# The opening of a decoder layer on one core: x's first row block in four transfers, weight casts on GpSimd, turning bank by bank, fewer products on ones, and one low weight computed earlier

## The chip, the core and the metric

The kernel runs on one core of one Trainium2 chip. Its engines work side by side and wait for each other by semaphores: TensorE (PE in the profile, with its weight loads as PEld), VectorE (DVE), ScalarE (ACT), GpSimd (POOL) and SyncE (SP), which issues most of the transfers; ScalarE and GpSimd issue some too. The metric is the device time of one execution in microseconds (us); the lower, the better.

## The reference: one hybrid decoder layer

One layer over 512 tokens of width 1024, all in float32. `u = rmsnorm(x)` is multiplied by a wide weight, and the product is split into the parts of three branches (dilated attention, causal pooling, a state-space scan) and their gates. The gated sum of the branches goes through `w_o` and onto x. A feed-forward part and a last norm end it:

```
u = rmsnorm(x, ln1_g)
proj = u @ w_in                                 # split into q, k, v, pool_in, z, xbc, dt_raw, gates
merged = gates[0] * y_a + gates[1] * y_b + gates[2] * y_c
x = x + merged @ w_o
h = causal_dwconv(rmsnorm(x, ln2_g) @ w_up)     # 2 x 2816 columns, 3 taps
x = x + (silu(a) * v) @ w_down                  # a and v are the two halves of h
return rmsnorm(x, final_g)
```

## The kernel before: split products, an opening by row blocks, orders written out by hand

**Products.** Every float32 factor is split into a high part (a rounded copy, tiles `wh`, `xh`, `uh`) and a low part (the rest, `wl`, `xl`, `ul`). A product is then three sums: high by high, low by high, high by low. `cast` makes the high part of a weight from the loaded tile `raw`, and `low` the low part: a subtraction on VectorE, line 217, 128x2048 numbers at a time.

**Order.** Each engine runs its instructions in the order in which the code writes them. `program` yields jobs, one for each piece of weights. While the body of a job runs, `prepare` makes the low part of the next job's weights, casts those of the one after and loads those after that. For a job marked `late`, `prepare` is not run ahead of the body but handed to it as a generator, `rest`: its first step is `low`, its second the cast and the load.

**The opening.** x is turned (its columns brought to the partitions) in four row blocks `tb` of 128 tokens. `load_x` loads a block in two halves `xin[tb, h]` of 512 columns. `turned` transposes the block's eight pieces of 128 columns with the unit matrix `eye`. Piece `k` goes to a PSUM tile: for blocks 0, 2 and 3 the pieces `k` and `k + 4` share one of four banks; block 1 has three tiles of its own (`uT1`, `first[2]`, `first[1]`). `split_x` reads each piece twice: ScalarE writes the high part `xh[k]` (line 1906) and VectorE the low part `xl[k]` (line 1907). The products with the first weight tile `raw0` start on blocks 0 and 1 together (256 tokens): `group(0, (HH,), 0, 256)` needs `xh` and the high part `h0`, the next group needs `xl`, and the groups with `LH` need `l0`, which GpSimd computes (`low0`). In profile rows these products have line 1918 and the names `pa<-xh,wh`, `pa<-xl,wh` and `pa<-xh,wl`. Ahead of the first transposition and behind those of block 1, `warm_up` puts products of a tile of ones with itself on TensorE, whose result nobody reads: `WARM` of them and `STILL` of them.

**The opening of the feed-forward part.** The first two jobs on `w_up` (`opening`, `half` 0 and 1) multiply the first 256 tokens while the norm of the last two row blocks is still under way. `late[0]` and `late[1]` are generators for row blocks 2 and 3: the rest of the norm (lines 475 to 483) and then `norm_turn` (transpositions, line 457; `uh` on ScalarE, line 460; `ul` on VectorE, line 461).

Of the kernel before, what the change touches and what calls it, by code (L numbers as in the profile page):

```python
# [16 lines left out]
P = 128  # L17
S = 512
D = 1024
KD = D // P  # L20
# [62 lines left out]
def trunk(ctx: ExitStack, tc, out, x, rel_bias, ln1_g, w_in, b_gate, w_a, pool_w, pool_scale, w_b,  # L83
# [3 lines left out]
    act, dve, pool, pe, sp = nc.scalar, nc.vector, nc.gpsimd, nc.tensor, nc.sync  # L87

    x, w_in, w_a, w_b, w_c, w_o = x[0], w_in[0], w_a[0], w_b[0], w_c[0], w_o[0]
# [16 lines left out]
    def T(name, dt=F32, shape=(P, S)):  # L106
        return big.tile(list(shape), dt, name=name, tag="t")

    def MM(name):
        return psum.tile([P, S], F32, name=name, tag="mm")  # L110

    def SM(name):
        return psum.tile([P, S], F32, name=name, tag="sm")

    def small(name, shape, dt=F32):
        return tiny.tile(list(shape), dt, name=name, tag="tiny")
# [38 lines left out]
    def step():  # L155
        flush()
        if waiting:
            running.append(iter(waiting.pop(0)))
        now = [(it, 0) for it in running]
        for phase in (0, ROWS, WHOLE, REST):  # L160
            now = [(it, advance(it, phase) if at == phase else at) for it, at in now]
# [65 lines left out]
    def wsrc(w, k0, k1, c0, c1):  # L227
        return w[k0 * P:k1 * P, c0:c1].rearrange("(k p) c -> p k c", p=P)
# [14 lines left out]
    def chunk_a(ps, ws, j, xh, xl, ks, lo=0, hi=S, k0=0):  # L243
        wh, wl = ws
        mm3(ps[:, lo:hi], lambda k: wh[:, k0 + k, j * P:(j + 1) * P],
            lambda k: wl[:, k0 + k, j * P:(j + 1) * P],
            lambda k: xh(k)[:, lo:hi], lambda k: xl(k)[:, lo:hi], ks)
# [1204 lines left out]
    def up_evac(m, ps):  # L1452
        t = HC[m] = T("hc")
        act.activation(t, ps, AF.Identity, bias=ff["c1"][:, ff["b"] + m:ff["b"] + m + 1], scale=fw(2, m))  # L1454
        for k in range(2):
            sh = 2 - k
            dve.scalar_tensor_tensor(t[:, sh:], ps[:, :S - sh], fw(k, m), t[:, sh:], OP.mult, OP.add)  # L1457
        if m < KF:
            act.activation(t, t, AF.Silu)  # L1459
            return  # L1460
        a = HC[m - KF]
        pool.tensor_tensor(a, a, t, OP.mult)  # L1462

        def later():
            yield
            k = m - KF
            if k % 2:
                h, l = T("fh", F32R), T("fl", F32R)
                act.copy(h, a)
                it = sums_of(HC[k - 1], a, T("sah", F32R), T("sal", F32R),  # L1470
                             lambda j, h, l: FS.__setitem__((j, k // 2), (h, l)), k >= KS)
                next(it)
                dve.tensor_sub(l, a, h.bitcast(F32))
                ACTS[k] = (h, l)
                yield
                for _ in it:
                    yield
                return
            t = T("f0", F32R)
            act.copy(t[:, :256], a[:, :256])  # L1480
            dve.tensor_sub(t[:, 256:], a[:, :256], t[:, :256].bitcast(F32))
            FS[0, k // 2] = (t[:, :256], t[:, 256:])

        running.append(later())
# [61 lines left out]
    def up_jobs():  # L1546
        held, rest = [], []

        def opening(job, half):
            def body(ws):  # L1550
                uh2, ul2 = nxt["uh"], nxt["ul"]
                if half == 0:
                    rest.append(job.prepare(later=True))
                    next(late[1])
                pss = [MM("pu") for _ in range(2)]

                def product(a, b, i):
                    for j in range(2):
                        for k in range(KD):
                            pe.matmul(pss[j][:, :256], a[:, k, j * P:(j + 1) * P], b[:, k, :256],  # L1560
                                      start=i + k == 0, stop=i == 2 and k == KD - 1)

                product(ws[0], uh2, 0)
                product(ws[0], ul2, 1)
                if half == 0:
                    product(ws[1], uh2, 2)
                next(late.pop(0), None)

                next(rest[0], None)
                if half:  # L1570
                    product(ws[1], uh2, 2)
                for j in range(2):
                    held.append((ws, j, pss[j], KF * half + j))
                if half == 0:
                    return
                for n, (ws_, j, ps, m) in enumerate(held):
                    chunk_a(ps, ws_, j, lambda k: uh2[:, k, :], lambda k: ul2[:, k, :], range(KD), 256, S)
                    if n == 1:
                        job.prepare()
                    up_evac(m, ps)  # L1580
                    step()
            return body

        for p in range(KF // 2):
            for half in range(2):
                def body(ws, p=p, half=half):
                    uh2, ul2 = nxt["uh"], nxt["ul"]
                    for j in range(2):
                        ps = MM("pu")
                        chunk_a(ps, ws, j, lambda k: uh2[:, k, :], lambda k: ul2[:, k, :], range(KD))  # L1590
                        up_evac(KF * half + 2 * p + j, ps)
                        step()
                c = half * DFF + p * 256
                job = Job([wsrc(w_up, 0, KD, c, c + 256)], KD, 256, body)
                if p == 0:
                    job.late = True
                    job.body = opening(job, half)
                yield job
# [233 lines left out]
    xin, warm = {}, small("warm", [P, 1])  # L1832

    def load_x(tb, engs=(sp, sp)):
        for h in range(2):
            t = xin[tb, h] = T("xin")
            engs[h].dma_start(t, x[tb * P:(tb + 1) * P, h * S:(h + 1) * S])
# [1 line left out]
    g8, g1 = T("g8"), cpool.tile([P, KD], F32, name="g1")  # L1839
    act.dma_start(g8[:KD, :P], ln1_g[0].rearrange("(k p) -> k p", p=P))  # L1840
    sp.dma_start(eye, c_eye)
    load_x(0, (act, sp))
    dve.memset(ones.bitcast(F32), 1.0)
    dve.memset(eps, EPS)
    dve.memset(both, 0.0)
# [11 lines left out]
    raw0 = w0.raw = wraw.tile([P, KD, 256], F32, name="raw", tag="raw")  # L1857
# [19 lines left out]
    h0 = w0.high = whp.tile([P, KD, 256], F32R, name="wh", tag="wh")  # L1877
# [3 lines left out]
    def part(j, k0, k1):  # L1881
        return slice(None), slice(k0, k1), slice(j * P, (j + 1) * P)

    def low0(j, k0, k1):
        o = part(j, k0, k1)
        pool.tensor_tensor(l0[o], raw0[o], h0[o].bitcast(F32), OP.subtract)
# [6 lines left out]
    def block(tb, k):  # L1893
        if tb == 1:
            return (uT1, first[2], first[1])[k % 3][:, (k // 3 + 1) * P:(k // 3 + 2) * P]
        return bank(k)[:, tb % 2 * P:tb % 2 * P + P]

    def turned(tb):
        if tb % 2 == 0:
            banks[:] = [SM("uT") for _ in range(4)]  # L1900
        for k in range(KD):
            pe.transpose(block(tb, k), xin[tb, k // 4][:, (k % 4) * P:(k % 4 + 1) * P], eye)

    def split_x(tb, k):
        c = slice(tb * P, (tb + 1) * P)
        act.mul(xh[k][:, c], block(tb, k), g1[:, k:k + 1])
        dve.scalar_tensor_tensor(xl[k][:, c], block(tb, k), g1[:, k:k + 1],
                                 xh[k][:, c].bitcast(F32), OP.mult, OP.subtract)
# [33 lines left out]
    warm_up(WARM)  # L1942
    pe.transpose(first[2][:, :KD], g8[:KD, :P], eye[:KD, :KD])
    turned(0)
    dve.tensor_copy(g1, first[2][:, :KD])
    for k in range(KD):
        split_x(0, k)
    turned(1)
    for k in range(KD):
        if k == 2:  # L1950
            for k0 in (0, 4):
                dve.tensor_copy(h0[part(0, k0, k0 + 4)], raw0[part(0, k0, k0 + 4)])
            low0(0, 0, KD)
        split_x(1, k)
    warm_up(STILL, 0)
    group(0, (HH,), 0, 256)
# [6 lines left out]
    half_squares(dve, 0, 1)  # L1963
    group(1, (HH,), 0, 256)
    turned(2)
    for k in range(KD):
        split_x(2, k)
# [79 lines left out]
AT = ((9, 10, 11, 12, 13, 14, 15), (17, 17, 18, 19, 20, 21, 22))  # L2047
MIX = "ZZ0zz1ggggwaa"
SSD_ORDER = ((0, 0, 1), (1, 0, 1), (0, 1, 1), (2, 0, 1), (1, 1, 1), (3, 0, 1), (2, 1, 1), (3, 1, 1))
WARM, STILL = 10, 7  # L2050

# [1 line left out]
_INS = ['x', 'rel_bias', 'ln1_g', 'w_in', 'b_gate', 'w_a', 'pool_w', 'pool_scale', 'w_b',  # L2053
# [26 lines left out]
```

## Time and profile before

| | |
|---|---|
| median of 3 runs | 1012.55 us (1012.4 to 1013.15) |
| the profiled execution | 1012.54 us, its span 1010.8 us |
| TensorE busy | 999.7 us, 99% of the span |
| VectorE, ScalarE, GpSimd busy | 753.7, 534.7 and 137.8 us |
| granted clock of TensorE over the span | 0.998 |

The profiled execution's own time is 1.7 us more than its span (what lies ahead of the first and behind the last instruction). It stands within 0.01 us of the median of the runs. A row of a timeline gives the start, the time from the first start to the last end of the merged instructions, the engine, the line, what is written from what, and, in brackets, the time for which the engine sat idle before it and who ended that.

### The profile page before, as it was taken

Reading aid. Unit: us, or ns where it says so; the run is one execution under the profiler, and the core shown is the slowest. Engines: PE = TensorE matmul, PEld = TensorE weight load, DVE = VectorE, ACT = ScalarE, POOL = GpSimd, SP = SyncE. Lnnn points to the kernel's source line nnn. Section 1 sums busy time; section 2 is a strip of 40 time slices with the busy share of each in tenths; the row PEclk is TensorE's granted clock in tenths of the full one; section 3 lists DMA queues with packets and bytes.
Section 4 is the critical chain, followed back from the end, with each engine's and each line's share of the span. In section 5 each row is a group of like instructions: output and inputs, shape, how many; then the busy total and the mean of one; then the engine's idle time right before and its main releaser. Section 6 shows DMA issues by size and latency. Waiting matters only on the chain.

```text
span 1010.8 us, 13607 instructions
## 1 busy us (share of the span) xinstructions
PE 999.7 (99%) x5307; PEld 850.0 (84%) x5307; DVE 753.7 (75%) x962; ACT 534.7 (53%) x929; POOL 137.8 (14%) x111
## 2 busy tenths in 40 slices
PE   9999999999999999999999999999999999999996
PEld 8898878999988888888888888898888888888885
DVE  6995668677767645776889888868778768685877
ACT  6343546554445566888566246554444434443456
POOL 4400010110000000000044501302111100121032
PEclk9999999999999999999999999999999999999999
DMA  7344360755343435552254754232352134542573
GB/s 221 102 126 131 106 187 4 193 150 147 102 155 94 108 100 132 146 137 62 77 152 125 211 188 90 80 126 84 99 193 84 50 117 149 175 115 73 146 184 109
DMA packets 117735, 127.03 MB, mean 126 GB/s; under 512 B 6791, under 2 KB 96462, under 8 KB 117671
## 3 DMA queue, kind: packets, MB, share of 16 engines
q1 hardware_dynamic: 112327, 116.98, 37.4%
q0 software_dynamic: 5040, 8.65, 5.4%
q8 instruction: 42, 0.69, 0.3%
q10 hardware_dynamic: 304, 0.53, 0.1%
q14 instruction: 22, 0.18, 0.1%
HBM read 121.56 MB, written 3.00 MB: 123 GB/s over the span
## 4 chain that ended last, share of the span: by engine, by line
PE 96%; DVE 2%; ACT 0%; DMA 0%; issue 0%; ACTq 0%
PE pa L239 37%; PE pu L239 23%; PE pb L239 10%; PE pd L239 8%; PE pqk L239 6%; PE pq L239 3%; PE ps L810 1%; PE pa L1918 1%; PE ppw L239 1%; PE po L858 1%; PE pt L844 1%; PE py L1140 1%; DVE wl L217 1%; PE pyo L1147 1%; PE pst L1128 0%; DMA xin<-in_x_dram 0%
## 5 line engine op out<-in xcount | busy, mean ns | idle before, releaser
L217 DVE TENSOR_TENSOR wl<-raw,wh 128x2048 fp32r<-128x2048 f32 (+3 forms) x86 | 205.9, 2396 | 32.9 <-ACT wh L195 24.2
L195 ACT CAST wh<-raw 128x1024 fp32r<-128x1024 f32 (+2 forms) x168 | 167.0, 1011 | 53.0 <-DVE raw L362 17.8
L1457 DVE SCALAR_TENSOR_TENSOR hc<-pu,fcol,hc 128x510 f32<-128x510 f32 x88 | 65.9, 748 | 53.7 <-ACT hc L1454 52.0
L239 PE MATMUL pu<-uh,wh 128*128 128x512 f32 (+1 forms) x352 | 83.6, 379 | 0.0
L239 PE MATMUL pu<-uh,wl 128*128 128x512 f32 (+1 forms) x352 | 83.5, 379 | 0.0
L239 PE MATMUL pu<-ul,wh 128*128 128x512 f32 (+1 forms) x352 | 83.5, 379 | 0.0
L239 PE MATMUL pa<-uh,wh 128*128 128x512 f32 (+1 forms) x336 | 80.9, 380 | 0.0
L239 PE MATMUL pa<-ul,wh 128*128 128x512 f32 (+1 forms) x336 | 78.9, 374 | 0.0
L239 PE MATMUL pa<-uh,wl 128*128 128x512 f32 (+1 forms) x336 | 78.8, 374 | 0.0
L239 PEld LDWEIGHTS pu<-ul,wh 128*128 128x128 f32 x352 | 64.2, 188 | 12.5
L239 PEld LDWEIGHTS pu<-uh,wl 128*128 128x128 f32 x352 | 64.2, 188 | 12.4
L239 PEld LDWEIGHTS pu<-uh,wh 128*128 128x128 f32 x352 | 64.1, 188 | 12.4
L1454 ACT ACTIVATE hc<-pu,fcol,fcol 128x512 f32<-128x512 f32 x40 | 31.2, 779 | 75.7 <-PE pu L239 75.7
L239 PEld LDWEIGHTS pa<-ul,wh 128*128 128x128 f32 x336 | 60.7, 188 | 11.4
L239 PEld LDWEIGHTS pa<-uh,wl 128*128 128x128 f32 x336 | 60.7, 188 | 11.2
L239 PEld LDWEIGHTS pa<-uh,wh 128*128 128x128 f32 x336 | 59.4, 189 | 10.6
L1462 POOL TENSOR_TENSOR hc<-hc 128x512 f32<-128x512 f32 x22 | 29.9, 1360 | 279.0 <-DVE hc L1457 243.3
L217 DVE TENSOR_TENSOR wl<-w,wh 128x2048 fp32r<-128x2048 f32 (+1 forms) x26 | 54.3, 2088 | 9.8 <-issue 4.5
L195 ACT CAST wh<-w 128x1024 fp32r<-128x1024 f32 (+1 forms) x52 | 47.2, 950 | 8.6 <-DMA w<-in_ffn_w_down_dram 3.8
L832 ACT ACTIVATE sb<-sb,nmls 128x128 f32<-128x128 f32 (+1 forms) x72 | 30.0, 418 | 32.5 <-DVE nmls L829 21.9
L1459 ACT ACTIVATE hc<-hc 128x512 f32<-128x512 f32 x22 | 13.9, 633 | 40.3 <-DVE hc L1457 40.3
L1123 POOL TENSOR_TENSOR st<-st,dts 128x512 f32<-128x512 f32 x4 | 4.2, 1051 | 225.4 <-ACT st L1131 164.9
(461 smaller groups left out, 2012.8 us busy)
## 6 DMA issues: line engine op xcount, KB each, us to landing
raw<-in_w_in_dram SPq DMA_DIRECT2D x24, 1024.0 KB, 5.5
raw<-in_ffn_w_up_dram SPq DMA_DIRECT2D x22, 1024.0 KB, 5.1
raw<-in_w_in_dram SPq DMA_DIRECT2D x14, 512.0 KB, 4.0
raw<-in_w_in_dram SPq DMA_DIRECT2D x8, 768.0 KB
raw<-in_ffn_w_down_dram SPq DMA_DIRECT2D x6, 1024.0 KB, 4.9
raw<-in_w_b_dram SPq DMA_DIRECT2D x4, 1024.0 KB
al<-ad SPq DMA_DIRECT2D x16, 256.0 KB, 7.9
raw<-in_w_c_dram SPq DMA_DIRECT2D x4, 1024.0 KB, 5.3
```

Of the source, the lines that this page charges most:

```text
L195: (other.tensor_copy if other and i else act.copy)(job.high[:, :, o], job.raw[:, :, o])
L217: (eng or dve).tensor_tensor(l[:, :, o], job.raw[:, :, o], h[:, :, o].bitcast(F32), OP.subtract)
L239: pe.matmul(ps, l, r, start=first and n == 0, stop=last and n == total - 1, skip_group_check=onto)
L810: pe.matmul(pss[i][:, o:o + w * P], q[r, n * P:(n + 1) * P], k[r, kb * P:(kb + w) * P], start=True, stop=True)
L832: act.activation(sb[:, off:off + w * P], sb[:, off:off + w * P], AF.Exp, bias=nm[:, n, h:h + 1], accum_out=ls[:, n, h:h + 1])
L844: pe.transpose(pt[:, o:o + P], sb[:, o:o + P], eye)
L858: pe.matmul(po[DH * hh:DH * hh + DH, n * P:(n + 1) * P], V[g, kb + i][:, (2 * c + hh) * DH:(2 * c + hh + 1) * DH], probs[2 * c + hh, nb][: ...
L1140: pe.matmul(py[DH * i:DH * i + DH, j * P:(j + 1) * P], xc[:, o:o + DH], als[j // 2][:, lo:lo + P], start=True, stop=True)
L1454: act.activation(t, ps, AF.Identity, bias=ff["c1"][:, ff["b"] + m:ff["b"] + m + 1], scale=fw(2, m))
L1457: dve.scalar_tensor_tensor(t[:, sh:], ps[:, :S - sh], fw(k, m), t[:, sh:], OP.mult, OP.add)
L1459: act.activation(t, t, AF.Silu)
L1462: pool.tensor_tensor(a, a, t, OP.mult)
```

## The change

The edits of the opening: the two halves of x's row block 0 are each loaded in two transfers of 256 columns, first the first 256 columns of both halves, then the second, ScalarE issuing those of half 0 and SyncE those of half 1. `turned` goes through the pieces in the order 0, 4, 1, 5, 2, 6, 3, 7, so that the two pieces of a bank follow each other. The high part of the first half of `raw0` is made by GpSimd instead of VectorE, ahead of all of block 1's splitting. `WARM` goes from 10 to 7 and `STILL` from 7 to 4. In the feed-forward opening the first step of `rest` (the low part of the second job's weights) moves from behind the products of `half` 0 to ahead of them.

```
     if half == 0:
         rest.append(job.prepare(later=True))
+        next(rest[0])
         next(late[1])
...
     next(late.pop(0), None)
-    next(rest[0], None)
     if half:
+        next(rest[0], None)
         product(ws[1], uh2, 2)
...
-    load_x(0, (act, sp))
+    for c in (0, 256):
+        for h, eng in enumerate((act, sp)):
+            if c == 0:
+                xin[0, h] = T("xin")
+            eng.dma_start(xin[0, h][:, c:c + 256], x[:P, h * S + c:h * S + c + 256])
...
-        for k in range(KD):
+        for k in (0, 4, 1, 5, 2, 6, 3, 7):
             pe.transpose(block(tb, k), xin[tb, k // 4][:, (k % 4) * P:(k % 4 + 1) * P], eye)
...
     turned(1)
+    for k0 in (0, 4):
+        pool.tensor_copy(h0[part(0, k0, k0 + 4)], raw0[part(0, k0, k0 + 4)])
+    low0(0, 0, KD)
     for k in range(KD):
-        if k == 2:
-            for k0 in (0, 4):
-                dve.tensor_copy(h0[part(0, k0, k0 + 4)], raw0[part(0, k0, k0 + 4)])
-            low0(0, 0, KD)
         split_x(1, k)
...
-WARM, STILL = 10, 7
+WARM, STILL = 7, 4
```

TensorE at the start of the program, before (`uT` without a number and `pa` are PSUM tiles; `pa<-ones` are the products on ones; the last row is the first group of real products):

```order
L1854 MATMUL pa<-ones 128x128 x10
L1943 MATMUL pa<-eye,g_110 128x8
L1902 MATMUL uT<-eye,xin 128x128 x8
L1902 MATMUL uT_123<-eye,xin 128x128
L1902 MATMUL pa<-eye,xin 128x128 x2
L1902 MATMUL uT_123<-eye,xin 128x128
L1902 MATMUL pa<-eye,xin 128x128 x2
L1902 MATMUL uT_123<-eye,xin 128x128
L1902 MATMUL pa<-eye,xin 128x128
L1854 MATMUL pa<-ones 128x128 x7
L1918 MATMUL pa<-xh,wh 128x256 x8
```

and now (line numbers are 4 or 5 higher behind the new lines):

```order
L1859 MATMUL pa<-ones 128x128 x7
L1948 MATMUL pa<-eye,g_110 128x8
L1907 MATMUL uT<-eye,xin 128x128 x8
L1907 MATMUL uT_125<-eye,xin 128x128
L1907 MATMUL pa<-eye,xin 128x128 x4
L1907 MATMUL uT_125<-eye,xin 128x128 x2
L1907 MATMUL pa<-eye,xin 128x128
L1859 MATMUL pa<-ones 128x128 x4
L1923 MATMUL pa<-xh,wh 128x256 x8
```

Six products on ones are gone, and block 1's pieces come in the new order; nothing is moved past the first real products.

VectorE at the same place, before, from the splitting of block 0 (`uT`) to the first sum of squares (line 445):

```order
L1907 SCALAR_TENSOR_TENSOR xl<-uT,g_111,xh 128x128 x8
L1907 SCALAR_TENSOR_TENSOR xl<-uT_123,g_111,xh 128x128
L1907 SCALAR_TENSOR_TENSOR xl<-pa,g_111,xh 128x128
L1952 CAST wh<-raw 128x4x128 x2
L1907 SCALAR_TENSOR_TENSOR xl<-pa,g_111,xh 128x128
L1907 SCALAR_TENSOR_TENSOR xl<-uT_123,g_111,xh 128x128
L1907 SCALAR_TENSOR_TENSOR xl<-pa,g_111,xh 128x128 x2
```

and GpSimd now, from the barrier of the program's start on:

```order
L2080 UNCONDITIONAL_BRANCH
L1955 CAST wh<-raw 128x4x128 x2
L1891 ISA
L1891 TENSOR_TENSOR wl<-raw,wh 128x8x128 x2
L1977 TENSOR_TENSOR xf<-xh,xl 128x256 x8
```

The two casts left VectorE, where they stood between the second and the third piece of block 1, and are GpSimd's first work; GpSimd's subtractions (line 1886 before) stand behind them as they stood first before.

VectorE at the opening of the feed-forward part, before (`va`, `vo`, `v`, `r`, `rt` and `u` are row block 3's norm; the first `ul` row is row block 2's, the second row block 3's; line 217 is the low part of the second job's weights):

```order
L1330 TENSOR_SCALAR va_106<-so_105 128x1
L1331 TENSOR_SCALAR vo_107<-va_106 128x1
L475 SCALAR_TENSOR_TENSOR v<-ss,vo_107 128x1
L476 RECIPROCAL r<-sq 128x1
L477 SCALAR_TENSOR_TENSOR rt<-r,v 128x1
L478 SCALAR_TENSOR_TENSOR rt<-rt,r 128x1
L482 SCALAR_TENSOR_TENSOR u_5961<-x_5515,rt,grow 128x512
L461 TENSOR_TENSOR ul_5789<-uT,uh_5788 128x4x128 x2
L217 TENSOR_TENSOR wl<-raw,wh 128x2048
L461 TENSOR_TENSOR ul_5789<-uT,uh_5788 128x4x128 x2
```

and now:

```order
L1330 TENSOR_SCALAR va_106<-so_105 128x1
L1331 TENSOR_SCALAR vo_107<-va_106 128x1
L217 TENSOR_TENSOR wl<-raw,wh 128x2048
L475 SCALAR_TENSOR_TENSOR v<-ss,vo_107 128x1
L476 RECIPROCAL r<-sq 128x1
L477 SCALAR_TENSOR_TENSOR rt<-r,v 128x1
L478 SCALAR_TENSOR_TENSOR rt<-rt,r 128x1
L482 SCALAR_TENSOR_TENSOR u_5957<-x_5511,rt,grow 128x512
L461 TENSOR_TENSOR ul_5785<-uT,uh_5784 128x4x128 x4
```

The subtraction moved up past the rest of row block 3's norm and past row block 2's `ul`; TensorE's order there is unchanged.

## The prediction

> **What bounds the kernel now.** I read the page first (its busy times and the chain that ended last), then TensorE's waits, then the chain and the timeline of the opening.
>
> ```profile
> span 1010.8 us, 13607 instructions
> PE 999.7 (99%) x5307; PEld 850.0 (84%) x5307; DVE 753.7 (75%) x962; ACT 534.7 (53%) x929; POOL 137.8 (14%) x111
> PE 96%; DVE 2%; ACT 0%; DMA 0%; issue 0%; ACTq 0%
> ```
>
> TensorE is the bound from end to end: 96% of the chain, 11.1 us of the span not busy. TensorE's waits say where an edit can act at all (us in total, times, longest):
>
> ```profile
> PE pa L1854 <- DVE ones L1843: 1.1, 1, 1.1
> PE pa L1918 <- ACT xh L1906: 0.8, 1, 0.8
> PE pu L1560 <- DVE wl L217: 0.6, 1, 0.6
> PE uT L1902 <- DMA xin<-in_x_dram: 0.5, 1, 0.5
> ```
>
> There are four, and the change aims at the last three: two in the first 11 us, one in the feed-forward opening at 666 us. Between and behind them TensorE has work, so what is saved there should stay saved to the end. The chain through the opening (start, length):
>
> ```profile
> 1.36 4.20 DMA xin<-in_x_dram
> ...
> 5.61 0.78 PE uT L1902 x5
> ...
> 6.41 0.38 ACT xh L1906
> ...
> 6.81 2.68 DVE xl L1907 x10
> 9.49 0.67 DVE wh L1952 x2
> 10.16 0.27 DVE xl L1907
> ...
> 10.46 0.38 ACT xh L1906
> ...
> 10.88 2.80 PE pa L1918 x19
> ```
>
> x lands, five transpositions pass before the first split (bank 0 is full only with piece 4), and VectorE's two casts of the weights hold up the splits behind them: ScalarE's next piece waits for VectorE. The timeline of the same stretch shows where TensorE comes to run without a pause:
>
> ```profile
> 9.41 0.76 DVE L1952 CAST wh<-raw 128x512 fp32r<-128x512 f32 x2
> ...
> 9.97 1.81 PE L1918 MATMUL pa<-xh,wh 128*128 128x256 f32 x8 [0.83 <-ACT xh L1906]
> 10.24 5.20 POOL L1886 TENSOR_TENSOR wl<-raw,wh 128x1024 fp32r<-128x1024 f32 x2 [9.80 <-DVE wh L1952]
> ...
> 10.46 0.37 ACT L1906 ACTIVATE xh<-pa,g 128x128 fp32r<-128x128 f32 x1 [0.56 <-DVE xl L1907]
> ...
> 11.50 1.01 PEld L1918 LDWEIGHTS pa<-xl,wh 128*128 128x128 f32 x8
> ```
>
> The eight products of the first group take 1.53 us from 9.97 to 11.50, though eight weight loads of the next group take 1.01 (0.12 each). From 11.50 on TensorE is full. So the first gain is how much earlier than 11.50 the second group starts.
>
> **Term 1, the opening: 0.93 us.** Three chains must meet there: the splits, the high part h0, and x's low parts.
>
> The splits start earlier. Pieces 0, 4, 1, 5 need half of the bytes that they needed, and the first split waits for two transpositions instead of five. I estimate the first split at 5.2 (6.41 before): half of the 4.20 us of the DMA row is latency that stays, the rest halves. From the first split to the second group it took 11.50 - 6.41 = 5.09 us, of which 0.56 was ScalarE's wait behind the casts, now gone; so the second group could start by 9.73. The fewer products on ones only keep TensorE free for x: fourteen passes instead of twenty end near 4.2 to 4.5 at the pace of the start (row under the clock's rival).
>
> h0 is later than that. It needs raw0's first half, whose landing the change doesn't hasten:
>
> ```profile
> 2.60 1.06 SPq L1860 DMA_DIRECT2D raw<-in_w_in_dram  x2
> raw<-in_w_in_dram SPq DMA_DIRECT2D x2, 512.0 KB, 6.0
> 4.00:6.00 2.00, 1.45 (x13) 1.24 (x13) 0.17 (x1) 0.00 (x0) 0.00 (x0) 1.00 1.01 372
> L1837 SPq DMA_DIRECT2D xin<-in_x_dram x7: 421/431/2937, 1.2 to 7.6; - x7
> ```
>
> Issued at 2.60, it lands 6.0 later, at 8.60. SyncE now issues one transfer more ahead of it (0.43), and so all behind it on that queue, x's blocks 1 to 3 among them. But from 4 us on the DMA engines are full (share 1.01, 372 GB/s) and the same bytes stand in front, so I take 8.7, from 8.5 to 8.9. GpSimd waits for it with nothing else queued, casts 2 times 128x512, and the fifth product needs the second cast. The trace has no cast on GpSimd. Bounds (busy us, mean ns; then VectorE's own casts of this shape, min/median/max ns):
>
> ```profile
> L1123 POOL TENSOR_TENSOR st<-st,dts 128x512 f32<-128x512 f32 x4 | 4.2, 1051 | 225.4 <-ACT st L1131 164.9 <-PE pst L1128 34.5 <-DVE xs L1153 26.1
> L1321 POOL TENSOR_TENSOR xg<-x,grow 128x512 f32<-128x512 f32 x4 | 9.2, 2299 | 16.7 <-DVE x L1376 16.7
> L1952 DVE CAST wh<-raw x2: 419/421/423, 9.4 to 9.7; 128x512 fp32r<-128x512 f32 x2
> ```
>
> So a cast costs c between 0.42 (VectorE's) and 2.30 (GpSimd's dearest group of this size, two inputs, beside a busy VectorE). I take 0.70: 1.05 of the cheapest group moves two streams in and one out, the cast one in and one out, two thirds. It is nearest to that row, since in this stretch VectorE reads PSUM for half of its input. The second group then starts at 8.7 + 2 x 0.70 + 4 x 0.12 = 10.57, and the gain is 11.50 - 10.57 = 0.93; in general 2.33 - 2c.
>
> What moves behind it is covered: GpSimd's two subtractions start at 10.1 and take 5.20, so l0's second half is there at 15.3, and TensorE wants it at 17.41 less the gains, about 16.2 (row below). ScalarE's casts of raw0's second half wait for its landing as before.
>
> **Term 2, turning by banks: 0.31 us.** Two row blocks of eight transpositions each, and the group behind:
>
> ```profile
> 13.52 1.04 PE L1902 MATMUL uT<-eye,xin 128*128 128x128 f32 x8
> 16.30 1.35 PE L1902 MATMUL uT<-eye,xin 128*128 128x128 f32 x8
> 17.41 1.20 PE L1918 MATMUL pa<-xh,wl 128*128 128x256 f32 x8
> ```
>
> Block 3 takes 1.35 against block 2's 1.04: it writes into the banks that block 2's splits are still reading, and the order 0, 1, 2, 3 wants the fourth bank after three transpositions. The new order wants it after six (0.33 later), and block 2's splits start three transpositions earlier. The 0.31 should go entirely; it is hidden in busy time and in no list of waits.
>
> **Term 3, the low weights: 0.64 us.** The feed-forward opening:
>
> ```profile
> 660.31 0.15 DVE L1331 TENSOR_SCALAR vo<-va 128x1 f32<-128x1 f32 x1
> 661.00 0.16 DVE L475 SCALAR_TENSOR_TENSOR v<-ss,vo 128x1 f32<-128x1 f32 x1 [0.54 <-ACT junk L443]
> 661.98 0.75 DVE L482 SCALAR_TENSOR_TENSOR u<-x,rt,grow 128x512 f32<-128x512 f32 x1
> 662.66 1.05 ACT L460 CAST uh<-uT 128x512 fp32r<-128x512 f32 x2
> 664.47 2.28 DVE L217 TENSOR_TENSOR wl<-raw,wh 128x2048 fp32r<-128x2048 f32 x1
> 665.13 1.04 PE L457 MATMUL uT<-eye,u 128*128 128x128 f32 x8
> 666.80 2.18 PE L1560 MATMUL pu<-uh,wl 128*128 128x256 f32 x16 [0.64 <-DVE wl L217]
> 668.82 1.12 PE L239 MATMUL pu<-uh,wh 128*128 128x256 f32 x8
> ```
>
> The subtraction now runs from 660.5 to 662.8. Queued behind it on VectorE is row block 3's norm (475 to 482): it starts 1.7 later and ends at 664.4 instead of 662.73. The transpositions that need it come at 665.13: 0.7 to spare, and without that cover each us there would be a us lost. ScalarE's uh for row block 2 stands behind row block 3's scaling and ends near 665.5 instead of 663.7; TensorE reads it from 668.2 on. The four ul rows end near 667.6, wanted at 669.1. So the wait goes, and nothing is late next. Bounds: 0 (if something else holds) to 0.64.
>
> **Sum.** 0.93 + 0.31 + 0.64 = 1.88 us. The profiled execution took 1012.54, the median is 1012.55: 1012.54 - 1.88 = 1010.66, so 1010.7.
>
> **The rivals.** *GpSimd casts as fast as VectorE.* With c = 0.42 term 1 is 1.49, the sum 2.44, the time 1010.1. For it: a cast has one input, and GpSimd's rows above all have two. Against: nothing of GpSimd's here runs at VectorE's pace. "GPSIMD Engine Reference" of the Trainium skill, section "Engine selection", says that work with two inputs is about twice as slow there as on VectorE and with one input runs roughly at line rate; no row here shows one input.
>
> *GpSimd becomes the bound and the kernel slower.* h0 is now GpSimd's alone. The sum is 3.28 - 2c; from c = 1.64 on it is a loss. At the 2.30 of line 1321 h0 is complete at 13.3, the second group starts at 13.8, term 1 loses 2.27, and the time is 1013.9. For it: the row of line 1321. Against: that has two inputs, and line 1886 with two inputs takes 2.6 us for twice the columns in this very stretch.
>
> *The clock falls.* TensorE's pace on the products on ones, at the start and from 3.96 on:
>
> ```profile
> 1.06 2.50 PE L1854 MATMUL pa<-ones 128*128 128x128 f32 x10 [1.06 <-DVE ones L1843]
> 3.96 0.94 PE L1854 MATMUL pa<-ones 128*128 128x128 f32 x7
> ```
>
> Ten passes in 2.50 at the start, seven in 0.94 later: twice the pace, reached after some 2.9 us of steady work. With seven products the steady stretch is 3.1 to 3.5 us, and from there to 10 us TensorE pauses for longer than before. If the pace falls there, some 2.9 us of the real products go at half pace: a loss of 1.4, time 1012.1. Against: the pauses before (0.55, 0.83) did nothing, and none now should pass 1.5 us. "TensorE: Matmul & The Clock Gate" of the Trainium skill, part 1, says that the clock halves after an idle window of about 3.4 us and that the windows run free of the kernel's start; by this the seven products are a near thing and the pauses are not. This trace's 2.9 us agree with a window that had begun before the kernel.
>
> *The opening's gain is given back* at a later wait that the shift uncovers, and terms 2 and 3 alone stay: 1011.6. Against: the list of TensorE's waits names none between 11 and 660 us.
>
> **How the numbers follow.** A change of 0.2% is 2.0 us, about what a measurement of this kernel can tell from no change; the forecast lies just inside. The sum passes 2.0 for c below 0.63. My case (all three terms, c from 0.55 to 0.9, landing 8.5 to 8.9) has 0.50: times from 1010.2 to 1011.3, of it 0.22 beyond the bound and 0.28 within. Casts at VectorE's pace: 0.23, faster. GpSimd as the bound: 0.12, of it 0.08 within and 0.04 slower. The clock: 0.10, of it 0.07 within and 0.03 slower (two such stretches, or one with dear casts). Given back: 0.05, within. Faster 0.45, within 0.48, slower 0.07. The range runs from 1009.9 (casts at 0.42, landing at 8.5) to 1012.6 (the clock's 1012.1 with casts 0.25 dearer): only most of the GpSimd rival and the tail of the clock's lie above.
>
> **What would show it.** In the changed profile: GpSimd's cast rows of some 0.7 us from 8.7 on, the second group's weight loads near 10.6 instead of 11.50, with TensorE's only wait there on GpSimd; block 3's transpositions in 1.04; no wait of TensorE on line 217. The prediction is wrong if the casts take less than 0.5 or more than 1.0, if raw0 lands elsewhere than 8.5 to 8.9, if products of the first groups stand 0.2 apart, or if a wait of TensorE appears that is in no list of before.

## The result: 1.75 us faster, and the profile after

The changed kernel took 1011.08 us (median of 21 runs, 1010.25 to 1013.26), the kernel before 1012.83 (21 runs beside it, 1011.96 to 1013.89). The ratio is 0.9985, 95% interval 0.9979 to 0.9991: faster by 1.75 us, 0.17%, where 1.88 were forecast. Medians here and below are over all runs; the ratio is not the quotient of the two medians, which would be 0.9983.

The profiled execution took 1011.78 us, 0.70 more than that median; that of before lay 0.29 under its own. So the two profiles differ by 0.76 only, and I read them place by place. The page and TensorE's waits:

```profile
span 1010.0 us, 13587 instructions
PE 1000.0 (99%) x5295; PEld 850.4 (84%) x5295; DVE 754.0 (75%) x960; ACT 535.2 (53%) x929; POOL 137.7 (14%) x113
PE pa L1859 <- DVE ones L1848: 1.1, 1, 1.1
PE pa L1907 <- DVE xl L1912: 0.9, 1, 0.9
```

The waits on line 217 at the feed-forward opening and on the first transpositions are gone, but TensorE is not less busy: something runs slower. The timeline of the opening (start, first start to last end, engine, line):

```profile
4.54 2.20 PE L1907 MATMUL uT<-eye,xin 128*128 128x128 f32 x9
5.27 2.70 ACT L1911 ACTIVATE xh<-uT,g 128x128 fp32r<-128x128 f32 x8 [1.54 <-PE uT L1907]
7.65 1.08 PE L1907 MATMUL pa<-eye,xin 128*128 128x128 f32 x4 [0.91 <-DVE xl L1912]
9.17 1.77 PE L1859 MATMUL pa<-ones 128*128 128x128 f32 x8
9.20 0.37 ACT L1911 ACTIVATE xh<-uT,g 128x128 fp32r<-128x128 f32 x1 [1.24 <-PE uT L1907]
9.34 1.17 POOL L1955 CAST wh<-raw 128x512 fp32r<-128x512 f32 x2 [8.89 <-DMA raw<-in_w_in_dram]
10.67 1.02 PEld L1923 LDWEIGHTS pa<-xh,wh 128*128 128x128 f32 x8
11.04 0.36 ACT L1911 ACTIVATE xh<-pa,g 128x128 fp32r<-128x128 f32 x1
11.61 1.03 PEld L1923 LDWEIGHTS pa<-xl,wh 128*128 128x128 f32 x8
```

The first split comes at 5.27, 1.14 earlier than before, as planned, and GpSimd's two casts take 1.17 together. But block 1 of x is turned late, raw0 is there only at 9.34, and the second group starts at 11.61, later than the 11.50 of before. Eight passes on ones take 1.77, 0.22 apart, where 0.11 is the full pace: TensorE ran at half pace until 10.65 us. The row at 7.65 names VectorE as releaser, but VectorE's splits were then still under way; in the run e8_ones_0_0 below the same row, at 7.75, ends "[0.98 <-DMA xin<-in_x_dram]": so I put the wait down to the landing of block 1. The row at 11.04 is ScalarE's last split of block 1. It ends at 11.40, while in the profile of before,

```profile
10.98 0.36 ACT L1906 ACTIVATE xh<-pa,g 128x128 fp32r<-128x128 f32 x1
```

it ends at 11.34: the 1.14 that the first split gained were gone by then.

The other two places, block 3's transpositions and the second job's weight loads at the feed-forward opening:

```profile
16.45 1.04 PE L1907 MATMUL uT<-eye,xin 128*128 128x128 f32 x8
665.68 1.97 PEld L1561 LDWEIGHTS pu<-uh,wl 128*128 128x128 f32 x16
```

and the latter in the profile of before:

```profile
666.80 1.97 PEld L1560 LDWEIGHTS pu<-uh,wl 128*128 128x128 f32 x16 [0.88 <-DVE wl L217]
```

Block 3 takes 1.04, as forecast. The wait of 0.88 is gone without a new one. Matching the same weight load in both traces gives TensorE's shift against before: +0.13 us at 13, -0.17 at 17.4, -1.13 at 668, -0.80 at the end. So in this execution term 1 is 0.13 lost, term 2 is 0.30, term 3 is 0.96, and 0.33 go in the last group (weight loads of TensorE, after and then before):

```profile
999.10 0.53 PEld L239 LDWEIGHTS pb<-wl,fh 128*128 128x128 f32 x3 [0.53 <-DVE wl L217]
```

```profile
999.91 0.54 PEld L239 LDWEIGHTS pb<-wl,fh 128*128 128x128 f32 x3 [0.20 <-DVE wl L217]
```

### The profile page after: what moved, and what is told of

Its sections match the earlier page's. It is cut to its first block, busy times and chain, and to the rows that moved or that the text cites. A ratio compares the mean times of both kernels' runs of the same rounds, so it can differ in the third digit from the quotient of the medians.

```text
span 1010.0 us, 13587 instructions
## 1 busy us (share of the span) xinstructions
PE 1000.0 (99%) x5295; PEld 850.4 (84%) x5295; DVE 754.0 (75%) x960; ACT 535.2 (53%) x929; POOL 137.7 (14%) x113
## 3 DMA queue, kind: packets, MB, share of 16 engines
q0 software_dynamic: 5040, 8.65, 5.4%
## 4 chain that ended last, share of the span: by engine, by line
PE 95%; DVE 1%; issue 1%; ACT 1%; DMA 1%; POOL 0%; ACTq 0%; POOLq 0%
PE pa L239 37%; PE pu L239 23%; PE pb L239 9%; PE pqk L239 6%; PE pd L239 6%; PE pq L239 3%; PE ps L810 1%; PE pa L1923 1%; PE pu L1561 1%; PE ppw L239 1%; PE po L858 1%; PE pt L844 1%; PE py L1140 1%; DMA w<-in_ffn_w_down_dram 1%; PE pyo L1147 1%
## 5 line engine op out<-in xcount | busy, mean ns | idle before, releaser
L239 PEld LDWEIGHTS pa<-ul,wh 128*128 128x128 f32 x336 | 60.7, 188 | 11.4
L239 PEld LDWEIGHTS pa<-uh,wh 128*128 128x128 f32 x336 | 59.4, 189 | 10.6
```

Of the source, the lines that this page charges most:

```text
L239: pe.matmul(ps, l, r, start=first and n == 0, stop=last and n == total - 1, skip_group_check=onto)
```

## The experiments

**Theory A**: the opening yields its 0.9 us when x lands early and TensorE's pace doubles early; both were late in the profiled execution. **Rival B**: it never yields anything. From the first four runs came **theory C**: raw0's landing, which the four transfers delay, sets the second group; and for moving raw0, **rival D**: the DMA engines are shared, so another order only moves the wait. The table holds all runs; "cast" is the start of raw0's first cast (in before, e2, e3 and e5 on VectorE, where it stands behind splits, so that it is not raw0's landing), "2nd group" that of its weight loads, "shift" that of TensorE at 13 us against the profile of before, in us (for e8_ones_0_0, whose pace doubled late, at 15 us).

| run | median less before's | ratio (95%) | cast | 2nd group | shift |
|---|---|---|---|---|---|
| before | | | 9.41 | 11.50 | |
| changed | -1.75 | 0.9985 (0.9979 to 0.9991) | 9.34 | 11.61 | +0.13 |
| e1_after_again | -1.98 | 0.9983 (0.9974 to 0.9992) | 9.50 | 11.91 | +0.43 |
| e2_low_alone | -0.84 | 0.9989 (0.9980 to 0.9998) | 9.28 | 11.37 | -0.12 |
| e3_banks_alone | -0.31 | 0.9994 (0.9985 to 1.0003) | 9.78 | 11.88 | +0.39 |
| e4_open_alone | -0.46 | 0.9994 (0.9985 to 1.0003) | 9.78 | 11.46 | -0.03 |
| e5_casts_vector | -1.32 | 0.9989 (0.9980 to 0.9998) | 9.15 | 11.25 | -0.23 |
| e6_two_transfers | -1.56 | 0.9982 (0.9973 to 0.9991) | 8.65 | 11.39 | -0.10 |
| e7_ones_10_7 | -1.87 | 0.9983 (0.9975 to 0.9992) | 9.05 | 11.08 | -0.41 |
| e8_ones_0_0 | +0.38 | 1.0003 (0.9994 to 1.0012) | 9.48 | 11.81 | +2.11 |
| e9_raw0_scalar | +0.91 | 1.0005 (0.9996 to 1.0014) | 11.36 | 13.69 | +3.41 |
| e10_raw0_scalar_two | -0.20 | 0.9997 (0.9988 to 1.0006) | 9.14 | 12.27 | +0.79 |
| e11_two_10_7 | -1.86 | 0.9980 (0.9971 to 0.9988) | 8.81 | 10.97 | -0.52 |
| e12_tiles_block1 | -2.06 | 0.9979 (0.9970 to 0.9988) | 8.61 | 10.47 | -1.02 |

An interval is about 1.8 us wide, so the times alone do not resolve a single term; where the traces show a term, they decide. But each kernel has one trace, of one execution, and in the opening executions differ.

**The changed kernel again** (no edit):

> The changed kernel once more, as a second look at the opening. Theory A (the opening yields its 0.9 us when the first blocks of x land as early as in the profile of before and TensorE's pace doubles near 4 us; in the profiled execution both were late): in this profile the second group's weight loads start near 10.6 to 10.8 if the products of the first groups stand 0.11 apart, near 11.6 if they stand 0.21 apart; span 1009.0 to 1009.3 in the first case, 1010.0 in the second. Rival B (the opening yields nothing in any execution, because raw0 lands 0.7 later behind the extra transfer and the blocks of x behind it): the second group starts at 11.4 to 11.7 at either pace, raw0 lands at 9.3, span 1010.0. Both: wait of TensorE on line 217 gone near 666 us.

Measured: 1010.73, raw0 at 9.50, the second group at 11.91, span 1010.0. It decides nothing between A and B, since the pace failed again, in another way. The view by windows of this run, cut where the granted clock changed (length, busy us of TensorE and count, PEclk, DMA share, GB/s):

```profile
4.30:7.71 3.41, 1.84 (x11) 1.00 0.92 281
7.71:11.12 3.41, 3.35 (x16) 0.50 1.15 327
11.12:14.53 3.41, 3.41 (x31) 1.00 1.08 362
```

The clock had risen at 4.30 and fell at 7.71, behind a window in which TensorE was busy for 1.84 of 3.41 us: the passes on ones were over, block 0 was turned quickly, and block 1 was not there.

**The low weight alone.** Before plus:

```
     if half == 0:
         rest.append(job.prepare(later=True))
+        next(rest[0])
...
-    next(rest[0], None)
     if half:
+        next(rest[0], None)
```

> The kernel before with the one low weight moved up and nothing else. Theory A and rival B alike: TensorE stands as before up to 666 us, and from there on 0.88 us earlier (the idle time on PEld's row of before; by the 0.64 that the prediction took from PE's row it would be 0.64); at the end about 0.3 of it is given back in the last group, where a cast of weights waits for a transfer whose landing does not move. Span down 0.5 to 0.9. If the give-back comes from the opening's shift instead, nothing of the 0.88 is lost at the end.

Measured: TensorE's shift goes from -0.12 at 600 us to -1.02 at 668: 0.90, and all of it is there at the end. The second job's weight loads,

```profile
665.78 1.97 PEld L1561 LDWEIGHTS pu<-uh,wl 128*128 128x128 f32 x16
```

come without a wait, 1.02 earlier than before. The last group waits 0.20 on line 217, as before.

**The turning alone.** Before plus `for k in (0, 4, 1, 5, 2, 6, 3, 7)` in `turned`.

> The kernel before with the pieces turned in the order 0, 4, 1, 5, 2, 6, 3, 7 in every block and nothing else. Term 2 alone: block 3's transpositions 1.04 instead of 1.35, TensorE 0.31 earlier from 17.5 us on. In block 0 the first split could start after two transpositions, but both halves of x must then have landed whole, so it moves by three transpositions at most, 0.3 to 0.4 us; the second group's start stays at 11.5, since the casts on VectorE still stand ahead of block 1's third piece. If the first split's earlier start carries through, the second group starts 0.3 earlier and the whole is 0.6.

Measured: block 3's transpositions, in this run's timeline,

```profile
16.69 1.04 PE L1902 MATMUL uT<-eye,xin 128*128 128x128 f32 x8
```

take 1.04, and the shift goes from +0.39 at 13 us to +0.08 at 17.4: 0.31. The start of the second group, 0.38 later than before, is this execution's (pace doubled at 7.04 only).

**The opening's loads, casts and ones alone.** Before plus the four transfers, GpSimd's casts and `WARM, STILL = 7, 4`.

> The kernel before with block 0 in four transfers, the casts on GpSimd and 7 and 4 products on ones, in the old order of pieces and without the low weight moved. Theory A: with the early doubling of pace the second group starts near 10.6 to 10.9, 0.6 to 0.9 us earlier than before; with the late doubling near 11.6. Rival B: 11.4 to 11.7 at either pace. With pieces 0, 1, 2, 3 first, the first split waits for the fifth piece again: it starts near 6.2 rather than 5.3. Block 3's transpositions stay at 1.35 and the wait on line 217 stays; span 1010.0 to 1011.0.

Measured: the second group at 11.46, although the pace had doubled at 5.62. Theory A's 10.6 to 10.9 is refuted here: raw0 came at 9.78, not at 8.7.

```profile
9.78 1.17 POOL L1954 CAST wh<-raw 128x512 fp32r<-128x512 f32 x2 [9.34 <-DMA raw<-in_w_in_dram]
11.46 1.02 PEld L1922 LDWEIGHTS pa<-xl,wh 128*128 128x128 f32 x8
```

ScalarE's last split of block 1 ended at 10.48 in this run, so the second group did wait for h0: both casts end at 10.95, and the prediction's 0.48 behind that is 11.43. The landing is late for two things that the traces show. SyncE issues raw0 at 3.08 us with four transfers and at 2.60 with two; and the bandwidth between 5.0 and 6.5 us is lower (last figure of each row; before, changed, e6_two_transfers):

```profile
5.00:6.50 1.50, 0.95 (x9) 0.89 (x9) 0.17 (x1) 0.09 (x1) 0.00 (x0) 1.00 1.01 337
```

```profile
5.00:6.50 1.50, 1.50 (x9) 1.16 (x7) 0.70 (x2) 1.09 (x3) 0.00 (x0) 1.00 0.90 249
```

```profile
5.00:6.50 1.50, 1.06 (x5) 1.06 (x6) 0.00 (x0) 0.34 (x1) 0.00 (x0) 1.00 1.03 345
```

In the six traces with four transfers and raw0 in its old place it is 241 to 307 GB/s, in the six with two 310 to 366. In the five profiles with four transfers, GpSimd's casts and raw0 in its old place, raw0 is there at 9.05 to 9.78; in the three with two transfers and GpSimd's casts at 8.61 to 8.81. Why the rate sinks, the traces do not show.

**The casts back on VectorE**, all else as changed:

```
-    for k0 in (0, 4):
-        pool.tensor_copy(h0[part(0, k0, k0 + 4)], raw0[part(0, k0, k0 + 4)])
-    low0(0, 0, KD)
     for k in range(KD):
+        if k == 2:
+            for k0 in (0, 4):
+                dve.tensor_copy(h0[part(0, k0, k0 + 4)], raw0[part(0, k0, k0 + 4)])
+            low0(0, 0, KD)
         split_x(1, k)
```

> The changed kernel with the two casts of raw0 back on VectorE, between the second and third piece of block 1. Theory A (the casts on GpSimd carry the opening's gain, since ScalarE and VectorE no longer wait behind them): the second group starts 0.3 to 0.6 later than with GpSimd's casts at the same landing of raw0 (VectorE's splits stand 0.8 behind the casts, ScalarE's next piece 0.56), time 0.3 to 0.6 above the changed kernel's, about 1011.2. Theory C (the landing of raw0 sets the opening, and the casts cost 0.61 each on GpSimd against 0.42 on VectorE, so the two ways cancel): within 0.2 of the changed kernel.

Measured: 1011.47, 0.4 to 0.7 above the changed kernel's two medians, theory A's side. ScalarE waits for VectorE again (0.74 at 10.21 in this run's timeline). Since the intervals overlap, this is an indication, and a weak one: two of the five executions above 1011.5 us have a granted clock of 0.996 over the span, which belongs to the clock's rival (below) and not to the casts.

**Two transfers**, all else as changed: `load_x(0, (act, sp))` in place of the loop.

> The changed kernel with x's block 0 in two transfers as before. In the three profiles with four transfers so far raw0 is there for the cast at 9.3 to 9.8, in before at 8.6, and block 1's last packets end at 7.1 to 7.2, in the three with two transfers at 6.3 to 6.6. Theory C (the four transfers delay what stands behind them on SyncE's queue as much as they hasten block 0): here raw0's cast starts at 8.6 to 8.9, block 1's splits by 8.2, the second group at 10.6 to 11.0, and the time is equal to or up to 0.5 below the changed kernel's. Theory A (the landings were late by chance, the four transfers bring the first split forward by 1.1 and that is the gain): the first split at 6.0 to 6.4, the second group at 11.0 to 11.4, the time 0.3 to 0.6 above the changed kernel's.

Measured: raw0 at 8.65 as theory C said, but the second group at 11.39 and not at 10.6 to 11.0. Its timeline:

```profile
7.41 1.06 PE L1903 MATMUL pa<-eye,xin 128*128 128x128 f32 x4
8.65 1.17 POOL L1951 CAST wh<-raw 128x512 fp32r<-128x512 f32 x2 [8.20 <-DMA raw<-in_w_in_dram]
8.90 1.81 PE L1855 MATMUL pa<-ones 128*128 128x128 f32 x8
10.40 1.05 PEld L1919 LDWEIGHTS pa<-xh,wh 128*128 128x128 f32 x8
```

h0 is ready at 9.82, and the first group starts at 10.40: half pace (doubled at 10.49), and the products on ones stand in its way. Half pace stretched block 0's transpositions too, so ScalarE's last split of block 1 ended only at 11.14. Theory A's 11.0 to 11.4 is met, but not for its reason; theory C missed a further chain. The time is the changed kernel's within the interval: the four transfers are not what gains.

**More products on ones**: `WARM, STILL = 10, 7`, all else as changed.

> The changed kernel with 10 and 7 products on ones instead of 7 and 4. In two of the three profiles with 7 and 4, TensorE's pace was half when the first real products came (rise at 10.65 us; rise at 4.30, fall at 7.71, rise at 11.12). If the fewer products cause that: here the pace doubles by 4.3 or 7.7 and stays, the first groups' products stand 0.11 to 0.12 apart, and the time is 0 to 0.4 below the changed kernel's. If the pauses for x cause it (four transfers leave TensorE idle between blocks 0 and 1, 5.8 to 6.9): the pace still falls in one profile of two. If the ones stand in the way (half pace, 14 passes of 0.21 behind block 1): the first group starts 1.0 to 1.3 later than with 4, at 11.5 or more, and the time is 0.5 to 1.0 above. My own: equal within 0.3.

Measured: pace doubled at 6.68 and stayed, second group at 11.08, 1010.92: the same median, as I expected.

**None**: `WARM, STILL = 0, 0`.

> The changed kernel with no products on ones at all: TensorE is idle until x lands, so the pace must be half until the first groups. It prices the clock's rival: the products of the first groups stand 0.21 apart until the pace doubles, 3 to 4 us after the first group's start; 14 to 16 products at half pace cost 1.5 to 1.7 more than at full pace, less what the first group waits for h0 anyway (0.4 to 0.8): the time is 0.8 to 1.6 above the changed kernel's if that runs mostly at full pace, and within 0.4 of it if it runs mostly at half pace already.

Measured: 1013.17, 2.1 to 2.4 above the changed kernel, more than expected. The timeline, with the pace doubling at 15.84:

```profile
10.14 2.08 PE L1923 MATMUL pa<-xh,wh 128*128 128x256 f32 x8 [0.66 <-POOL wh L1955]
12.02 1.91 PE L1923 MATMUL pa<-xl,wh 128*128 128x256 f32 x8
13.73 1.91 PE L1923 MATMUL pa<-xh,wh 128*128 128x256 f32 x8
```

Three groups ran at 1.91 to 2.08 instead of 1.12, not two. Half pace in the first three groups thus cost over 2 us here, and some ones are needed.

**raw0 on ScalarE's queue** (its definition and `load_w0`, with `eng=sp` as a parameter, moved up behind x's block 0; the second run with two transfers as well):

```
+    load_w0(0, 0, 8, act)
     dve.memset(ones.bitcast(F32), 1.0)
...
     load_x(1)
-    load_w0(0, 0, 8)
     load_w0(1, 0, 8)
```

> The changed kernel with the first half of raw0 issued by ScalarE's queue, right behind its two transfers of x, instead of by SyncE behind block 1. Theory C (the landing of raw0 sets the opening: with four transfers its cast starts at 9.05 to 9.78, and the second group stands 2.0 to 2.4 behind it): the cast starts at 7.5 to 8.3, the second group is bound by block 1's splits instead, at 10.2 to 10.8, and the time is 0.4 to 1.0 below the changed kernel's. Rival D (the DMA engines are shared: what raw0 gains, block 1 of x loses, and the clock's state decides): block 1 lands 0.5 to 1.0 later, first split of block 1 at 9.3 or more, the second group at 11.3 to 12, the time within 0.3 of the changed kernel's or above it.

> As the run before, with x's block 0 in two transfers. Theory C: raw0's cast starts at 7.5 to 8.3, block 1's splits start at 8.2 to 8.9 as in the kernel before, the second group at 10.2 to 10.8; equal to the run before within 0.3. Rival D: with block 0 whole, raw0 shares the DMA engines with both blocks; the first split at 6.4 to 6.8 and the second group at 11.3 to 11.8, the time 0.2 to 0.6 above the changed kernel's.

Measured: 1013.62 and 1012.51. Issued some 0.9 us earlier, raw0 landed later: 2.0 later than in the changed kernel in the first run, 0.5 later than in e6_two_transfers in the second. The first run's timeline:

```profile
8.62 0.63 PE L1907 MATMUL pa<-eye,xin 128*128 128x128 f32 x4 [0.76 <-DMA xin<-in_x_dram]
9.51 0.37 ACT L1911 ACTIVATE xh<-uT,g 128x128 fp32r<-128x128 f32 x1 [1.43 <-PE uT L1907]
11.36 1.16 POOL L1955 CAST wh<-raw 128x512 fp32r<-128x512 f32 x2 [10.92 <-DMA raw<-in_w_in_dram]
```

Theory C's forecasts fail in both runs. Rival D has the direction right and not the size: it had raw0 gain what block 1 loses, with the second group at 11.3 to 12 and 11.3 to 11.8, and it came at 13.69 and 12.27. Both block 1 and raw0 come later, and in both runs the pace fell (at 9.59 and at 8.01). A transfer that is issued earlier need not land earlier; how much of the times is the landing's and how much the clock's, these runs do not separate.

**Two transfers, 10 and 7 products on ones:**

> The changed kernel with x's block 0 in two transfers and 10 and 7 products on ones, so that of the opening's edits only GpSimd's casts and the order of pieces are left. If the casts carry the gain of the opening (removing them cost 0.4 to 0.7 in the medians) and the four transfers and fewer products on ones do not (removing each cost 0.2 or less beyond the noise): 1010.8 to 1011.2, as the changed kernel, and in the profile the pace doubles at or before 7.7, the second group at 10.6 to 11.0. If four transfers are what is worth it: 1011.4 to 1011.8.

Measured: 1010.85. Of the opening's edits only the casts and the order of pieces are left, and nothing is lost.

**And block 1 turned tile by tile**, in `turned`:

```
-        for k in (0, 4, 1, 5, 2, 6, 3, 7):
+        for k in ((0, 3, 6, 1, 4, 7, 2, 5) if tb == 1 else (0, 4, 1, 5, 2, 6, 3, 7)):
```

> The run before this one (two transfers, 10 and 7 products on ones) with block 1's pieces turned tile by tile of its own three tiles: 0, 3, 6, 1, 4, 7, 2, 5. In the changed kernel's profile ScalarE's first split of block 1 comes only behind the seventh transposition, at 9.20, since pieces 0, 3 and 6 share a tile. Theory (ScalarE's chain of splits sets the second group once raw0 lands early): the first split of block 1 no longer waits where the blocks land late; where ScalarE comes from block 0's splits without a pause, nothing changes. Gain 0 to 0.3, so 1010.6 to 1010.9. Rival: no effect, 1010.85 within 0.2, because ScalarE is never idle there with two transfers.

Measured: 1010.68, the lowest of all, 0.17 below the run before it and not to be told from that by the intervals. Its timeline is the opening as forecast:

```profile
6.04 2.43 ACT L1907 ACTIVATE xh<-uT,g 128x128 fp32r<-128x128 f32 x9 [2.79 <-PE uT L1903]
8.30 0.69 ACT L1907 ACTIVATE xh<-pa,g 128x128 fp32r<-128x128 f32 x2
8.61 1.17 POOL L1951 CAST wh<-raw 128x512 fp32r<-128x512 f32 x2 [8.17 <-DMA raw<-in_w_in_dram]
9.28 1.27 PEld L1919 LDWEIGHTS pa<-xh,wh 128*128 128x128 f32 x8 [0.21 <-POOL wh L1951]
9.95 0.36 ACT L1907 ACTIVATE xh<-pa,g 128x128 fp32r<-128x128 f32 x1
10.47 1.02 PEld L1919 LDWEIGHTS pa<-xl,wh 128*128 128x128 f32 x8
```

raw0 at 8.61, ScalarE without a pause from block 0 to block 1, the second group at 10.47. But the rival, no effect, is the better reading: in e11_two_10_7 ScalarE had no pause there either. From its first split to the end of its last it took 4.26 there and 4.27 here; the whole chain only began 0.51 earlier, since the pace doubled at 5.14 instead of 6.38.

## Why the prediction was right, and where its steps were not

The forecast of 1010.7 stands 0.4 from the median, and the difference of 1.88 is 0.13 from the measured 1.75. It is right in part by luck: two errors of opposite sign cancel. And two of the signs that it named for being wrong came true: raw0 landed elsewhere than at 8.5 to 8.9, and a wait of TensorE appeared (0.9 on line 1907) that is in no list of before.

**Term 2** (0.31) is exact: in all eleven profiles with the new order TensorE gains 0.30 to 0.32 between 13 and 17.4 us (in e8_ones_0_0 from 15 us on).

**Term 3** was mis-sized: 0.64 forecast, 0.90 to 0.97 in the eleven profiles that have the edit. The step that failed is the row: the 0.64 is the idle time before the products, whose ends are modelled, while the weight loads waited 0.88. Row block 3's norm had the cover claimed: its transpositions, moved up with all else, came without a wait.

**Term 1** was too large: 0.93 forecast. From the medians, 1.75 and 1.98 less 0.31 and 0.93 leave 0.5 to 0.7. In the profiled executions it is nothing (0.13 and 0.43 lost). Four of its steps, as they stood:

"whose landing the change doesn't hasten ... so I take 8.7, from 8.5 to 8.9" failed: 9.05 to 9.78 with four transfers. raw0 was issued 0.48 later, and the bytes in front did not flow as fast.

"so the second group could start by 9.73" failed too. It carries the earlier first split through ScalarE's whole chain of splits, and the chain broke at block 1: in the changed kernel ScalarE waited 1.24 us for block 1's transpositions. From its first split to the end of its last it took 6.13 there, against 4.93 before (and 5.18 in e3, with the new order of pieces and VectorE's casts). Where block 1 was there in time and GpSimd cast (e4, e7, e11, e12), it took 4.26 to 4.49: so moving the casts does shorten this chain, by 0.4 to 0.7 us, and the four transfers can lengthen it again.

"0.70" per cast was good. From the changed kernel's trace, by line:

```profile
L1955 POOL CAST wh<-raw x2: 609/612/614, 9.3 to 9.9; 128x512 fp32r<-128x512 f32 x2
```

0.61 against VectorE's 0.42. The Trainium skill, "GPSIMD Engine Reference", section "Engine selection", has work with one input roughly at line rate; here it takes 1.45 times as long as on VectorE, and the rival built on 0.42 falls. So does GpSimd as the bound: that needed 1.64.

"h0 is later than that" made h0 the only bound. The rule that the second group starts at raw0 plus both casts plus 0.48 holds in e4_open_alone (11.43 for 11.46), where ScalarE was done early. It gives 8.61 + 1.17 + 0.48 = 10.26 for e12_tiles_block1, where the second group started at 10.47, 0.16 behind the end of ScalarE's last split. In seven of the fourteen traces (before, e2, e3, e5, e7, e11, e12) it starts 0.16 behind that end: there ScalarE's chain is the bound. For the changed kernel the rule gives 10.99, and ScalarE's chain 11.40 + 0.16 = 11.56, where it was 11.61: block 1's transpositions came late and at half pace, and the passes on ones held the first group until 10.67, behind h0 at 10.51.

**The clock's rival** (chance 0.10) took place in part. Half pace reached the opening in both profiles of the changed kernel: in the first the pace only rose late (10.65), in e1_after_again it fell, at 7.71, as the rival has it. But the first real products ran at full pace in the first and mostly so in the second, so the loss is not the 1.4 of the rival. I had argued that no pause passes 1.5 us. The Trainium skill, "TensorE: Matmul & The Clock Gate", part 1, has the clock halve after an idle window of about 3.4 us; here it halved behind windows in which TensorE was busy for 1.84, 1.71 and 1.22 of 3.41 us, so an idle window is not needed. Without a profile there is no record of when the clock changed, but each execution has its granted clock over the span. Executions above 1011.5 us are 10 of 32 with the changed kernel and 1 of 44 in the four kernels with two transfers, or 10 and 7 on ones, or both. Seven of the ten have a granted clock of 0.995 or 0.996, as e1_after_again's profile with its fall has (0.996); none of the 22 below 1011.5 us has less than 0.997. So for seven of the ten the tail is the clock. The profiled execution is an eighth, with its late rise, which the span's clock doesn't count; two stay open.

**Given back later**: the 0.33 in the last group is no answer to the shift. Some 0.3 is also lost there in e4_open_alone, whose TensorE is 0.09 late, and nothing in e7_ones_10_7, 1.69 early. What decides it stays open.

So the gain is the low weight (0.9), the turning (0.3) and some half a microsecond of the casts on GpSimd. The first two are shown by traces with the edit alone. The last is argued, from the medians and from ScalarE's shorter chain; no run has the casts alone. The four transfers and the fewer products on ones gain nothing that could be measured, and the tail above 1011.5 us goes with having both.

## What to carry to other kernels

Where a first group waits for several chains (data, weights, the engine's own pace), speeding one up shows nothing until you know the next one; take a bound from each, and expect the landing of a transfer to move when those ahead of it are cut in pieces, or when it goes to another queue. Read the wait of weight loads rather than that of the products for the price of a late weight. Repeat the profile of an edit at a program's start, since the pace and the landings there differ from one execution to the next by as much as the edit.

## What the runs showed of the hardware that was not expected

The granted clock changed only at multiples of 3.41 us from one another, at a phase that differs by execution (before at 3.93 us, the changed kernel at 10.65, e8_ones_0_0 at 15.84). At full pace, windows with 2.21 us or more of TensorE's work kept it, and windows with 1.22 to 1.84 lost it in the opening. At the program's end three windows with 1.48 to 1.62 kept it (changed kernel, e10, e11), so the busy time as the trace gives it does not alone decide a fall. At half pace, windows busy for 2.75 and 2.91 us did not raise it, and windows of 2.87 (in another execution) and 3.00 did, so the limit lies near 2.9, or 85%, as far as busy times are read that closely. And ahead of the first change that a trace records, the column PEclk reads 1.00, though the spacing of the products shows half pace: there the pace is read from the rows.
